# Attention values and exponential sums on one NeuronCore: which operand stands in TensorE and which one moves

## The chip, the cores and the metric

The kernel runs on one NeuronCore of a Trainium2 chip. The metric is the device time of one execution in microseconds, as the median of several runs. Before the change it is 3464.32 us (three runs, 3463.7 to 3466.15).

## The reference, cut to what matters

Two layers of a trunk with three parallel branches (a convolution branch, grouped attention, a long convolution) and a channel mixer. The change concerns the attention of the 1024 latent tokens: 8 heads of 64, 2 groups of keys and values, 1024 own keys and 128 cached ones.

```
def _blocked_attention(q, k, v):
    b, lq, h, d = q.shape
    g = h // N_KV_HEADS
    nb = lq // Q_BLOCK
    qb = q.reshape(b, nb, Q_BLOCK, N_KV_HEADS, g, d).transpose(1, 0, 2, 3, 4, 5)
    scale = d ** -0.5
    def one_block(qi):
        s = jnp.einsum('bqkgd,bskd->bkgqs', qi, k, preferred_element_type=jnp.float32) * scale
        p = jax.nn.softmax(s, axis=-1).astype(v.dtype)
        return jnp.einsum('bkgqs,bskd->bqkgd', p, v)
```

All numbers are fp32. The result of the attention is half of the input of the output projection w_o.

## The kernel before

Activations lie with channels on the 128 partitions and the 1152 tokens (128 context tokens, then 1024 latent ones) in the free dimension. Each layer has four phases: `phase1` (norm, input projection, long convolution), `phase2` (attention, with the convolution branch and the modulation products of later stages beside it), `phase3` (output projection `wo`) and `phase4` (channel mixer `up`, `dn`). The large products of phases 1, 3 and 4 split each fp32 operand into a high and a low part and take three products.

`phase2` (line 1245) opens the pools and calls `attention` (line 1359). Four head pairs `j` (two heads `u` of one key group), two halves of 512 queries and nine chunks `c` of 128 keys make 72 chunks a layer, 144 in all. For one chunk:

- `st`: four products give the scores of 128 keys by 2 x 512 queries, with the row maximum already subtracted through extra rows of the stationary operand; tile `st`, two PSUM banks.
- `p`: one ScalarE exponential over 128 x 1024 (line 1388).
- `av`: `drain` (line 1363) runs two chunks behind. For each head and each block of 128 queries P stands (128 x 128) and the values move: 64 columns and a column of ones, so that column 64 collects the sum of the exponentials. That is eight fp32 products a chunk, accumulated over nine chunks in two PSUM banks.

After chunk 8 `finish` (line 1405) takes the two banks: on VectorE a reciprocal of the sums and a multiplication for each head, then four transposes on TensorE (tile `avt`) bring channels back to the partitions, and `mix_out` (line 1031) splits the result into high and low (ScalarE, VectorE) and stores it to the DRAM buffer `mixD`, from which phase 3 loads it. There are 16 finishes.

Beside this run, as generators that are advanced once a chunk: `maxes` (line 1313) for the next head pair (score products `S`, maxima `mx` on VectorE, transposes `mxt`), `prompt_attention`, `tapped_conv` (the 31-tap convolution on VectorE, ScalarE and GpSimd, then `mu`, `s`, `cr`, `pw` on TensorE) and `mod` (line 352: `cpad` with 32 columns stands, the modulation weights move, four products side by side; tile `modp`). `bcast64` (line 495) makes rows out of columns with pairs of products whose stationary block has 64 columns (tiles `cr`, `nr`).

All products go through one helper (`mm`, line 234), so rows of the profile are told apart by tiles. An fp32 product appears as two matmul instructions in the profile and as one in the program's order. The order of instructions on each engine is set by a scheduler when the program is built (it simulates the time line), not by the order of the lines alone. SP issues nearly all DMAs, in order.

Of the kernel before, what the change touches and what calls it, by code (L numbers as in the profile page):

```python
# [9 lines left out]
F32 = mybir.dt.float32  # L10
# [39 lines left out]
def _constants():  # L50
# [49 lines left out]
        cs[d, 1] = cs[d + 64, 1] = -s if d % 32 < 16 else s  # L100
    c["rope"] = cs.reshape(128, 2 * L)

    m = np.zeros((128, 260), np.float32)
    m[:, :128] = np.eye(128)
    m[:64, 128:192] = 1.0 / 64
    m[64:, 192:256] = 1.0 / 64
    m[:64, 256] = 1.0
    m[64:, 257] = 1.0
    m[:, 258:260] = 1.0 / DM
    c["cst"] = m  # L110
    return c

# [20 lines left out]
class Kern:  # L133
# [171 lines left out]

    def setup(self):
        nc, i = self.nc, self.i
        cst = self.one.tile([128, 260], F32, name="cst")
        nc.sync.dma_start(cst[:], i["cst"])
        self.ident, self.blk, self.sel, self.inv1k = cst[:, :128], cst[:, 128:256], cst[:, 256:258], cst[:, 258:260]  # L310
        self.eps = self.one.tile([128, 2], F32, name="eps")
        nc.vector.memset(self.eps[:, 0:1], EPS)
        nc.vector.memset(self.eps[:, 1:2], 64 * EPS)
        cd = self.one.tile([128, 16], F32, name="cd")
        nc.sync.dma_start(cd[:], i["cond"])
        self.vec = []
# [928 lines left out]
    def phase2(self, l, mods):  # L1245
        nc = self.nc
        with ExitStack() as ctx:
            tp = self.pool(ctx, f"tp{l}", 1)
            self.ap = self.pool(ctx, f"at{l}", 1)
            kp = self.pool(ctx, f"v{l}", 1)  # L1250
            main = {"m": self.pool(ctx, f"g{l}", 5), "t": self.pa}
            side = {"m": self.pool(ctx, f"gc{l}", 3), "t": self.pa}
            self.use(main)
            wm = self.pool(ctx, f"wm{l}", 3)
            self.sq = self.psum(ctx, f"s{l}", 1)

            V = self.V = kp.tile([128, 18, 65], F32, tag="v", name="vt")
            nc.gpsimd.memset(V[:, :, 64:65], 1.0)
            nc.sync.dma_start(V[:, 0:16, 0:64], self.vD[:].rearrange("p a b e -> p (a b) e"))
            nc.sync.dma_start(V[:, 16:18, 0:64], self.i["cv"][l].rearrange("p (b e) -> p b e", b=2))  # L1260
            bgs = [self.stream(self.prompt_attention(l, kp), side), self.stream(self.tapped_conv(l, tp, self.cp), side)]
            if mods is not None:
                bgs.append(self.stream(mods(wm), side))
            self.attention(l, bgs)
            for b in bgs:
                for _ in b:
                    pass
        self.actx.close()
# [90 lines left out]
    def attention(self, l, bgs):  # L1359
# [3 lines left out]
        def drain(n):  # L1363
            while len(pend) > n:
                j, half, c, P = pend.pop(0)
                g = j // 2
                if c == 0:
                    acc[0] = [self.sq.tile([128, 512], F32, tag=f"av{u}", name="av") for u in range(2)]
                for u in range(2):
                    for k in range(4):  # L1370

                        self.mm(acc[0][u][:, 65 * k : 65 * k + 65], P[:, 512 * u + 128 * k : 512 * u + 128 * k + 128], V[:, 2 * c + g, :],
                                c == 0 and k == 0, c == 8 and k == 3)
                if c == 8:
                    fins.append(self.finish(l, j, half, acc[0]))

        Q = self.first
        for j in range(4):
            g = j // 2
            cur, mg, nxt = Q, self.maxes(j + 1) if j < 3 else iter(()), None  # L1380
            for half in range(2):
                for c in range(9):
                    S = self.sq.tile([128, 2, 512], F32, tag="st", name="st")
                    for k, (K, n) in enumerate(((K1[g], 128), (K2[g], 66))):
                        for u in range(2):
                            self.mm(S[:, u, :], K[:n, 128 * c : 128 * c + 128], cur[u][k][:n, 512 * half : 512 * half + 512], k == 0, k == 1)
                    P = ap.tile([128, 1024], F32, tag="p", name="p", bufs=4)
                    self.act(P[:], S[:].rearrange("p a b -> p (a b)"), AF.Exp)
                    nxt = next(mg, nxt)
                    pend.append((j, half, c, P))  # L1390
                    drain(2)
                    for f in fins:
                        next(f, None)
                    for b in bgs:
                        for _ in range(3 if 9 * half + c + 18 * j > 40 else 1):
                            next(b, None)
# [5 lines left out]
            for _ in f:  # L1402
                pass

    def finish(self, l, j, half, av):

        nc = self.nc
        O, rr = self.M("av"), self.small([128, 2, 4, 1], "rs")
        o = O[:].rearrange("p (k u e) -> p u k e", k=4, u=2)
        for u in range(2):  # L1410
            a = av[u][:, 0:260].rearrange("p (k e) -> p k e", e=65)
            nc.vector.reciprocal(rr[:, u], a[:, :, 64:65])
            self.mul(o[:, u], a[:, :, 0:64], rr[:, u].to_broadcast([128, 4, 64]))
        yield
        t = self.T("avt")
        for k in range(4):
            self.tr(t[:, 128 * k : 128 * k + 128], O[:, 128 * k : 128 * k + 128])
        self.mix_out(l, j, t[:], 128 + 512 * half, 640 + 512 * half)
        yield

    def taps(self, l, tp):
# [416 lines left out]
```

## Time and profile before

| | |
|---|---|
| median of the runs | 3464.32 us |
| the profiled execution's own time | 3458.15 us |
| its span | 3456.4 us |
| TensorE, matmul | 94% of the span, 18938 instructions |
| TensorE, weight load | 88% |
| VectorE | 60% |
| ScalarE | 34% |
| mean granted TensorE clock | 0.948 |
| `av` matmuls | 2304 instructions, busy 306.4 us, 285 ns each |
| `av` weight loads | 2304 instructions, busy 312.1 us, 206 ns each |

The profiled execution is one run with the hardware profiler on. Busy time is a union of intervals; a matmul's duration has the time in which its result travels through the array, so matmuls that follow each other overlap in the rows, and the pace is read from the starts. A granted clock of 1.00 is 2.4 GHz and 0.50 is 1.2 GHz.

### The profile page before, as it was taken

The numbers are of one execution on the slowest core, as the hardware profiler recorded it, in microseconds if no ns is written. First come the engines' busy times: TensorE is split into PE (matmuls) and PEld (weight loads), VectorE is DVE, ScalarE is ACT, GpSimd is POOL, SyncE is SP. The second block draws the span as 40 slices with busy tenths as digits, with TensorE's granted clock in tenths as the row PEclk, the third lists the DMA queues.
The fourth block names the chain that finished last, engine by engine and source line by source line (L and its number), as shares of the span: only waits on it lengthen the run. The fifth ranks groups of instructions, "written<-read, shape, count | busy, mean of one in ns | idle before, by whom it ended". The sixth has DMA issues, their size and how long they took to land. (4 is left out here: it accounts for less than half of the span.)

```text
span 3456.4 us, 47618 instructions
## 1 busy us (share of the span) xinstructions
PE 3238.0 (94%) x18938; PEld 3054.2 (88%) x18938; DVE 2074.1 (60%) x3301; ACT 1176.0 (34%) x1944; POOL 568.5 (16%) x498
## 2 busy tenths in 40 slices
PE   5988888999979999999998888989999999999997
PEld 3888866799979999999998888768999999999997
DVE  7877779522775455444566885875146554455556
ACT  3422333342343332233344323425225222333323
POOL 6645421000220000000014662300001000000002
PEclk8999978989989999999999898889999999999998
DMA  7564455434411111111114445433411111111112
GB/s 282 163 208 150 135 153 175 159 113 150 126 56 43 43 41 43 43 43 43 41 49 137 144 117 162 146 128 97 163 46 37 40 43 43 42 41 43 43 41 70
DMA packets 150106, 332.44 MB, mean 96 GB/s; under 512 B 21459, under 2 KB 57687, under 8 KB 143356
## 3 DMA queue, kind: packets, MB, share of 16 engines
q1 hardware_dynamic: 145180, 314.84, 28.6%
q0 software_dynamic: 4704, 14.55, 1.5%
q8 instruction: 150, 2.46, 0.3%
q14 instruction: 72, 0.59, 0.1%
HBM read 261.13 MB, written 68.19 MB: 95 GB/s over the span
## 5 line engine op out<-in xcount | busy, mean ns | idle before, releaser
L234 PE MATMUL up<-hl,whi 128*128 128x384 f32 (+1 forms) x2112 | 713.3, 338 | 4.2 <-DVE hl L223 2.9
L234 PE MATMUL up<-hh,whi 128*128 128x384 f32 (+1 forms) x2112 | 710.8, 338 | 3.7 <-ACT hh L208 2.8
L234 PE MATMUL up<-hh,wlo 128*128 128x384 f32 (+1 forms) x2112 | 712.5, 337 | 0.0
L211 DVE TENSOR_TENSOR wlo<-wraw,whi 128x512 fp32r<-128x512 f32 x296 | 204.5, 691 | 636.6 <-ACT whi L228 636.4
L228 ACT CAST whi<-wraw 128x512 fp32r<-128x512 f32 x362 | 224.1, 619 | 826.3 <-PE dn L234 358.2
L234 PEld LDWEIGHTS up<-hl,whi 128*128 128x128 f32 x2112 | 398.6, 189 | 6.4 <-DVE hl L223 4.7
L234 PEld LDWEIGHTS up<-hh,whi 128*128 128x128 f32 x2112 | 398.6, 189 | 4.4 <-ACT hh L208 3.2
L234 PEld LDWEIGHTS up<-hh,wlo 128*128 128x128 f32 x2112 | 398.6, 189 | 0.0
L223 DVE SCALAR_TENSOR_TENSOR xt<-dn,mod,xt 128x128 f32<-128x128 f32 (+2 forms) x704 | 332.3, 512 | 71.6 <-PE dn L234 71.5
L234 PE MATMUL dn<-gh,wlo 128*128 128x384 f32 (+1 forms) x1056 | 359.0, 340 | 0.0
L234 PE MATMUL dn<-gh,whi 128*128 128x384 f32 (+1 forms) x1056 | 357.2, 338 | 0.0
L234 PE MATMUL dn<-gl,whi 128*128 128x384 f32 (+1 forms) x1056 | 357.0, 338 | 0.0
L234 PEld LDWEIGHTS av<-vt,p 128*128 128x128 f32 x2304 | 312.1, 206 | 21.9 <-issue 5.2
L211 POOL TENSOR_TENSOR acc<-acc,sq 128x384 f32<-128x384 f32 x51 | 55.4, 1095 | 1626.0 <-ACT sq L208 1625.1
L223 DVE SCALAR_TENSOR_TENSOR fu<-pd,vec,fu 128x1154 f32<-128x1154 f32 (+2 forms) x192 | 253.9, 1323 | 91.9 <-ACT fu L208 89.3
L234 PE MATMUL av<-vt,p 128*128 128x65 f32 x2304 | 306.4, 285 | 2.2 <-DVE av L211 2.2
L234 PE MATMUL win<-hh,whi 128*128 128x384 f32 x768 | 270.3, 354 | 27.3 <-ACT raw L724 9.9
L234 PE MATMUL win<-hl,whi 128*128 128x384 f32 x768 | 269.9, 352 | 7.5 <-DVE hl L223 2.9
L234 PE MATMUL win<-hh,wlo 128*128 128x384 f32 x768 | 268.4, 350 | 0.8 <-POOL wlo L211 0.8
L1341 DVE TENSOR_REDUCE mx<-S 128x1 f32<-128x384 f32 x384 | 197.1, 550 | 75.5 <-PE S L234 74.8
L208 ACT ACTIVATE p<-st 128x1024 f32<-128x1024 f32 x144 | 147.3, 1023 | 252.7 <-PE st L234 213.5
L1632 ACT COPY pd<-up 128x384 f32<-128x384 f32 (+1 forms) x352 | 131.5, 400 | 240.2 <-PE up L234 240.2
(282 smaller groups left out, 5414.6 us busy)
## 6 DMA issues: line engine op xcount, KB each, us to landing
wmod<-in_w_mod SPq DMA_DIRECT2D x48, 1024.0 KB, 6.7
wraw<-in_w_up SPq DMA_DIRECT2D x176, 256.0 KB, 2.6
wraw<-in_w_dn SPq DMA_DIRECT2D x88, 256.0 KB, 2.6
wraw<-in_w_in SPq DMA_DIRECT2D x64, 256.0 KB, 2.8
q<-qD SPq DMA_DIRECT2D x48, 256.0 KB, 7.1
mh<-mixD SPq DMA_DIRECT2D x16, 576.0 KB, 4.3
ml<-mixD SPq DMA_DIRECT2D x16, 576.0 KB, 5.9
khD<-fK SPq DMA_DIRECT2D x16, 512.0 KB, 2.9
```

The costliest lines, as they stand in the source:

```text
L208: return self.nc.scalar.activation(out, in_, f, **k)
L211: return (eng or self.nc.vector).tensor_tensor(out, a, b, op=op)
L223: return (eng or self.nc.vector).scalar_tensor_tensor(out, a, s, b, op0=op0, op1=op1)
L228: self.nc.scalar.copy(hi, src)
L234: self.nc.tensor.matmul(out, l, r, start=start, stop=stop)
L1341: nc.vector.tensor_reduce(m3[:, k, s : s + 1], S[:, :384], op=ALU.max, axis=AX.X)
L1632: self.nc.scalar.copy(p[:, u + o : v + o], t[:, u - a : v - a])
```

## The change

The values stand now, 64 columns for one head, and the exponentials move, 512 columns at a time. The two heads of a pair write to the lower and the upper 64 partitions of one PSUM tile (`av`). The sums of the exponentials come from products of their own: a block of 32 columns of ones stands (one element of `eps`, broadcast), P moves, and head and parity of the chunk choose one of four bands of 32 partitions of a second tile (`avs`). The result has channels on the partitions already, so the transposes go. `finish` copies both tiles with ScalarE, and adds the two parities and takes the reciprocal of the sums: for 14 of 16 head pairs and halves by way of DRAM (the four rows are stored, read back as 128 x 8, inverted, stored, and read broadcast over 64 partitions), for the last of each layer with small products (`rs`, then `bcast64`, tile `orr`). P has five buffers instead of four.

```
-            V = self.V = kp.tile([128, 18, 65], F32, tag="v", name="vt")
-            nc.gpsimd.memset(V[:, :, 64:65], 1.0)
+            V = self.V = kp.tile([128, 18, 64], F32, tag="v", name="vt")
...
-                    acc[0] = [self.sq.tile([128, 512], F32, tag=f"av{u}", name="av") for u in range(2)]
+                    acc[0] = [self.sq.tile([128, 512], F32, tag=f"av{u}", name=n) for u, n in enumerate(("av", "avs"))]
+                o, sm = acc[0]
                 for u in range(2):
-                    for k in range(4):
-
-                        self.mm(acc[0][u][:, 65 * k : 65 * k + 65], P[:, 512 * u + 128 * k : 512 * u + 128 * k + 128], V[:, 2 * c + g, :],
-                                c == 0 and k == 0, c == 8 and k == 3)
+                    self.mm(o[64 * u : 64 * u + 64, :], V[:, 2 * c + g, :], P[:, 512 * u : 512 * u + 512], c == 0, c == 8)
+
+                if c % 2 == 0 and c < 8:
+                    acc[1] = P
+                else:
+                    for k, x in enumerate((acc[1], P) if c < 8 else (P,)):
+                        for u in range(2):
+                            r = 64 * k + 32 * u
+                            self.mm(sm[r : r + 32, :], self.ones, x[:, 512 * u : 512 * u + 512], c == 1, c == (7 if k else 8))
                 if c == 8:
-                    fins.append(self.finish(l, j, half, acc[0]))
+                    fins.append(self.finish(l, j, half, acc[0], j == 3 and half == 1))
...
-    def finish(self, l, j, half, av):
+    def finish(self, l, j, half, av, last):
 
         nc = self.nc
-        O, rr = self.M("av"), self.small([128, 2, 4, 1], "rs")
-        o = O[:].rearrange("p (k u e) -> p u k e", k=4, u=2)
-        for u in range(2):
-            a = av[u][:, 0:260].rearrange("p (k e) -> p k e", e=65)
-            nc.vector.reciprocal(rr[:, u], a[:, :, 64:65])
-            self.mul(o[:, u], a[:, :, 0:64], rr[:, u].to_broadcast([128, 4, 64]))
-        yield
-        t = self.T("avt")
-        for k in range(4):
-            self.tr(t[:, 128 * k : 128 * k + 128], O[:, 128 * k : 128 * k + 128])
-        self.mix_out(l, j, t[:], 128 + 512 * half, 640 + 512 * half)
+        O, S = self.M("av"), self.M("sums")
+        nc.scalar.copy(O[:], av[0][:])
+        nc.scalar.copy(S[:], av[1][:])
+        if last:
+            t = self.T("rs")
+            for k in range(4):
+                self.mm(t[:, 2 * k : 2 * k + 2], S[:, 128 * k : 128 * k + 128], self.sel4, True, True)
+            rr = self.small([128, 4, 2], "rs")
+            nc.vector.reciprocal(rr[:], t[:, 0:8].rearrange("p (k u) -> p k u", u=2))
+            R = self.bcast64(rr, 0, 4, "orr")
+        else:
+            d, e = self.dram([2, 2, 512], f"sums{l}{j}{half}"), self.dram([2, 512], f"sumr{l}{j}{half}")
+            nc.sync.dma_start(d[:].rearrange("a u x -> (a u) x"), S[0:128:32, :])
+            n = self.small([128, 2, 8], "ns")
+            for a in range(2):
+                nc.sync.dma_start(n[:, a], d[a].rearrange("u (p e) -> (u p) e", e=8))
+            yield
+            yield
+            self.add(n[:, 0], n[:, 0], n[:, 1])
+            nc.vector.reciprocal(n[:, 0], n[:, 0])
+            nc.sync.dma_start(e[:].rearrange("u (p e) -> (u p) e", e=8), n[:, 0])
+            R = self.M("orr")
+            for u in range(2):
+                nc.sync.dma_start(R[64 * u : 64 * u + 64, :], e[u : u + 1, :].to_broadcast([64, 512]))
+            yield
+            yield
+        self.mul(O[:], O[:], R[:])
+        self.mix_out(l, j, O, 128 + 512 * half, 640 + 512 * half)
         yield
```

The scheduler orders the program anew. On TensorE, late in the first layer's attention, one chunk after the other stands before the change as follows (`st` scores, `av` values; `p_` with its number is the P of the chunk):

```order
L234 MATMUL st_6700<-q1_5977,k1_3589 128x512
L234 MATMUL st_6700<-q1_5982,k1_3589 128x512
L234 MATMUL st_6700<-q2_5978,k2_3592 128x512
L234 MATMUL st_6700<-q2_5983,k2_3592 128x512
L234 MATMUL av_6707<-vt_4248,p_6684 128x65 x4
L234 MATMUL av_6708<-vt_4248,p_6684 128x65 x4
```

In the changed kernel two successive chunks at the same place stand so (`avs` is the tile of the sums, `eps` holds the ones):

```order
L236 MATMUL st_6467<-q1_5857,k1_3590 128x512
L236 MATMUL st_6467<-q1_5862,k1_3590 128x512
L236 MATMUL st_6467<-q2_5858,k2_3593 128x512
L236 MATMUL st_6467<-q2_5863,k2_3593 128x512
L236 MATMUL av_6495<-p_6459,vt_4249 64x512 x2
L236 MATMUL avs_6496<-p_6459,eps_71 32x512 x2
L236 MATMUL st_6488<-q1_5857,k1_3590 128x512
L236 MATMUL st_6488<-q1_5862,k1_3590 128x512
L236 MATMUL st_6488<-q2_5858,k2_3593 128x512
L236 MATMUL st_6488<-q2_5863,k2_3593 128x512
L236 MATMUL av_6495<-p_6472,vt_4249 64x512 x2
L236 MATMUL avs_6496<-p_6472,eps_71 32x512 x2
```

The code issues the sums of an even chunk together with those of the odd one after it; in the built order each chunk's two sums products stand right behind its own two value products. In the whole program they stand 141 times as two in a row and 6 times alone.

On SP's DMA queue, where a head pair's finish and the loads for the last head pair meet in the first layer, the order before is:

```order
L1038 DMA mixD0_107<-mh_5309 128x512
L1039 DMA mixD0_107<-ml_5310 128x512
L1546 DMA mh_6907<-mixD0_107 128x1152
L1547 DMA ml_6908<-mixD0_107 128x1152
L359 DMA wmod_5401<-in_w_mod 128x2048
L359 DMA wmod_5480<-in_w_mod 128x2048
L1321 DMA q1_5977<-qD_109 64x1024 x2
```

and in the changed kernel:

```order
L1324 DMA q1_5862<-qD_110 64x1024 x2
L1325 DMA q2_5863<-qD_110 64x1024
L1429 DMA sums011_5913<-sums_5910 4x512
L1432 DMA ns_5916<-sums011_5913 128x8 x2
L1437 DMA sumr011_5914<-ns_5916 128x8
L1440 DMA orr_5979<-sumr011_5914 64x512
L364 DMA wmod_5243<-in_w_mod 128x2048
L364 DMA wmod_5318<-in_w_mod 128x2048
L1440 DMA orr_5979<-sumr011_5914 64x512
L1043 DMA mixD0_108<-mh_6029 128x512
```

The store and the three kinds of loads of the sums are new, each of them depends on the one ahead of it, and loads of `wmod` stand behind them.

## Rows read from the trace of the kernel before

**Rows 1.** Busy time in six windows: us, PE, PEld, DVE, ACT, POOL, PEclk, DMA share, GB/s

```profile
465.00:600.00 135.00, 118.50 (x678) 92.76 (x677) 119.46 (x220) 49.08 (x72) 32.81 (x25) 0.84 0.46 160
600.00:752.00 152.00, 148.23 (x957) 121.85 (x957) 69.83 (x174) 57.42 (x80) 0.00 (x0) 0.90 0.44 151
752.00:811.00 59.00, 58.56 (x439) 54.95 (x438) 4.79 (x14) 22.65 (x23) 1.05 (x1) 1.00 0.22 72
2155.00:2290.00 135.00, 122.05 (x653) 90.58 (x651) 117.74 (x216) 49.03 (x75) 33.76 (x26) 0.79 0.46 157
2290.00:2424.00 134.00, 130.36 (x905) 113.29 (x906) 72.83 (x173) 56.95 (x79) 0.00 (x0) 0.96 0.30 98
2424.00:2486.00 62.00, 61.27 (x456) 57.42 (x455) 7.11 (x20) 23.25 (x24) 0.00 (x0) 0.99 0.31 111
```

**Rows 2.** The same windows, instructions of tile av alone: us, PE, PEld, DVE

```profile
600.00:752.00 152.00, 68.18 (x477) 68.03 (x477) 3.31 (x12) 0.90 0.44 151
752.00:811.00 59.00, 42.26 (x359) 42.84 (x358) 3.40 (x12) 1.00 0.22 72
...
2290.00:2424.00 134.00, 62.97 (x490) 63.63 (x490) 3.25 (x12) 0.96 0.30 98
2424.00:2486.00 62.00, 43.59 (x364) 44.39 (x364) 3.65 (x12) 0.99 0.31 111
```

**Rows 3.** Timeline of PE late in layer 0: start, us, instruction, count

```profile
770.16 1.18 PE L234 MATMUL st<-q,k 128*128 128x512 f32 x4
771.18 1.90 PE L234 MATMUL av<-vt,p 128*128 128x65 f32 x16
772.88 1.17 PE L234 MATMUL st<-q,k 128*128 128x512 f32 x4
```

**Rows 4.** Busy time in stretches with a granted clock of 0.50, columns of rows 1

```profile
488.50:509.00 20.50, 20.48 (x78) 17.58 (x79) 14.17 (x33) 5.52 (x11) 4.53 (x3) 0.50 0.00 0
...
590.90:607.90 17.00, 17.00 (x71) 13.51 (x70) 10.07 (x21) 1.55 (x2) 0.00 (x0) 0.50 0.44 139
683.00:686.40 3.40, 3.38 (x14) 2.80 (x14) 2.65 (x7) 1.51 (x3) 0.00 (x0) 0.50 0.00 0
730.80:751.30 20.50, 20.50 (x94) 19.66 (x93) 0.69 (x1) 3.10 (x4) 0.00 (x0) 0.50 0.80 300
...
2181.50:2202.00 20.50, 20.50 (x79) 17.62 (x78) 16.19 (x34) 5.26 (x10) 3.75 (x3) 0.50 0.01 1
...
2294.10:2304.40 10.30, 10.20 (x41) 6.79 (x41) 4.61 (x12) 1.07 (x2) 0.00 (x0) 0.50 0.54 166
```

**Rows 5.** Timeline at 730 us, with the idle time before it and its releaser

```profile
730.37 6.29 PE L234 MATMUL av<-vt,p 128*128 128x65 f32 x30 [1.73 <-DVE av L211]
```

**Rows 6.** Timeline of PE around modp, at 477 us and at 2317 us

```profile
476.69 1.06 PE L234 MATMUL modp<-wmod,cpad 128*32 128x512 f32 x8
...
2316.54 1.92 PE L234 MATMUL modp<-wmod,cpad 128*32 128x512 f32 x16
2318.39 0.62 PE L234 MATMUL S<-k,q 128*128 128x384 f32 x2
```

**Rows 7.** Timeline of PE around cr, at 2374 us

```profile
2372.30 2.12 PE L234 MATMUL av<-vt,p 128*128 128x65 f32 x18
2374.35 0.87 PE L234 MATMUL cr<-cst,csd 128*64 128x128 f32 x12
2375.16 3.12 PE L234 MATMUL av<-vt,p 128*128 128x65 f32 x26
```

**Rows 8.** Timeline of PE, two st groups with av and transposes avt between them

```profile
2435.54 1.17 PE L234 MATMUL st<-q,k 128*128 128x512 f32 x4
...
2438.64 1.17 PE L234 MATMUL st<-q,k 128*128 128x512 f32 x4
```

**Rows 9.** Tile modp: a ScalarE copy of 128 x 512 out of PSUM, ns min/median/max

```profile
L368 ACT COPY modm<-modp x6: 567/586/587, 29.6 to 2277.3; 128x512 f32<-128x512 f32 x6
```

**Rows 10.** Tile qp: small loads from DRAM, issue to landing

```profile
DMA to landing us min/median/max: 1.8/2.8/4.2
```

More of the change, by code (lines that the diff above doesn't have):

```diff
@@ L101, in _constants @@
     c["rope"] = cs.reshape(128, 2 * L)
-    m = np.zeros((128, 260), np.float32)
+    m = np.zeros((128, 262), np.float32)
     m[:, :128] = np.eye(128)
@@ L109, in _constants @@
     m[:, 258:260] = 1.0 / DM
+    m[0:128:64, 260] = 1.0
+    m[32:128:64, 261] = 1.0
     c["cst"] = m
@@ L307, in setup @@
         nc, i = self.nc, self.i
-        cst = self.one.tile([128, 260], F32, name="cst")
+        cst = self.one.tile([128, 262], F32, name="cst")
         nc.sync.dma_start(cst[:], i["cst"])
         self.ident, self.blk, self.sel, self.inv1k = cst[:, :128], cst[:, 128:256], cst[:, 256:258], cst[:, 258:260]
-        self.eps = self.one.tile([128, 2], F32, name="eps")
+        self.sel4 = cst[:, 260:262]
+        self.eps = self.one.tile([128, 3], F32, name="eps")
         nc.vector.memset(self.eps[:, 0:1], EPS)
         nc.vector.memset(self.eps[:, 1:2], 64 * EPS)
+        nc.vector.memset(self.eps[:, 2:3], 1.0)
+        self.ones = self.eps[:, 2:3].to_broadcast([128, 32])
         cd = self.one.tile([128, 16], F32, name="cd")
@@ L1255, in phase2 @@
             self.sq = self.psum(ctx, f"s{l}", 1)
-            V = self.V = kp.tile([128, 18, 65], F32, tag="v", name="vt")
-            nc.gpsimd.memset(V[:, :, 64:65], 1.0)
-            nc.sync.dma_start(V[:, 0:16, 0:64], self.vD[:].rearrange("p a b e -> p (a b) e"))
-            nc.sync.dma_start(V[:, 16:18, 0:64], self.i["cv"][l].rearrange("p (b e) -> p b e", b=2))
+            V = self.V = kp.tile([128, 18, 64], F32, tag="v", name="vt")
+            nc.sync.dma_start(V[:, 0:16, :], self.vD[:].rearrange("p a b e -> p (a b) e"))
+            nc.sync.dma_start(V[:, 16:18, :], self.i["cv"][l].rearrange("p (b e) -> p b e", b=2))
             bgs = [self.stream(self.prompt_attention(l, kp), side), self.stream(self.tapped_conv(l, tp, self.cp), side)]
@@ L1386, in attention @@
                             self.mm(S[:, u, :], K[:n, 128 * c : 128 * c + 128], cur[u][k][:n, 512 * half : 512 * half + 512], k == 0, k == 1)
-                    P = ap.tile([128, 1024], F32, tag="p", name="p", bufs=4)
+                    P = ap.tile([128, 1024], F32, tag="p", name="p", bufs=5)
                     self.act(P[:], S[:].rearrange("p a b -> p (a b)"), AF.Exp)
```

## The prediction

> **What bounds the kernel now.** I read the windows of the attention phase first. The change touches that phase alone, once per layer: about 465 to 811 us and 2155 to 2486 us of the span. In the first 135 us of each, VectorE is busy 119.46 and 117.74 us, about 88%: row maxima and the tapped convolution. After that it falls to 70 of 152 us and 5 of 59, and TensorE has the stretch: 148 of 152, 59 of 59, 130 of 134, 61 of 62 us [rows 1]. So the phase has a part paced mostly by VectorE and a part paced by TensorE. The same windows for the tile av say how much of the work lies in the second part: 477, 359, 490 and 364 instructions [rows 2]. A chunk (128 keys for one head pair and 512 queries) has 8 products of two instructions each, so 16: 1690 / 16 = 105.6 of the 144 chunks are paced by TensorE, and 38.4 are not.
>
> The timeline of TensorE shows one chunk where nothing else runs: st starts at 770.16, av at 771.18, the next st at 772.88 [rows 3]. A chunk costs 1.02 + 1.70 = 2.72 us: four 512-column score products, then 16 av instructions with 65 columns moving. The exponential has slack there, at 1.02 us of 2.72.
>
> Last the clock: the granted clock is 0.50 (1.2 GHz) over several stretches inside the phase while TensorE is busy [rows 4]. One of them follows a wait of 1.73 us for VectorE to free the av sums [rows 5].
>
> **The change part by part.** *Values.* Per chunk the 16 instructions with P standing become two products with 64 columns of V standing and P moving, 512 columns each. A product is again two instructions, so 4. Their nearest relative is modp (fp32, 512 columns moving, 32 standing, four products side by side): 8 instructions take 1.06 us and 16 take 1.92 [rows 6]. So a full set of neighbours passes once in 0.86 / 2 = 0.43 us, and a product needs two passes. That 64-column neighbours also run together shows in cr: 12 instructions of 128 columns in 0.87 us [rows 7]; one after another at 0.11 each (a quarter of 0.43) they would need about 1.3 us before the tail of the last. So the av pair costs two passes.
>
> *Sums.* The diff speaks of blocks of 32 ones, four side by side. The scheduled order shows something else: after each av pair stand two sums products of the same P, 141 times "x2" and 6 singles in the whole program, never four. The block for the earlier P is moved ahead of the next av. Two products alone also need two passes, so the sums cost 0.86 us in every chunk, not in every second one.
>
> *Switching.* Going from 128 columns to 128, the next group starts 0.16 to 0.20 us before the last one's end: 771.34 against 771.18, and 773.08 against 772.88 [rows 3]. Between blocks of different width it starts only 0.07 before: 2318.46 against 2318.39 out of modp [rows 6], 2374.42 against 2374.35 into cr and 2375.22 against 2375.16 out of it [rows 7]. A chunk now has three such borders: 128 to 64, 64 to 32, 32 to 128. The trace has no border of 64 to 32; I bound it by 0.07 and 0.16 of overlap and take 0.07, since all borders between widths look so. The Trainium skill (TensorEngine Tiling, Key Properties) says that changing the tiling mode drains the engine, which would hold for 64 to 32 as well; that speaks against this change.
>
> *The chunk after.* st 1.18 - 0.07 = 1.11; av 1.06 - 0.07 = 0.99, and some 0.03 for the wider block to load; sums 1.06 - 0.07 = 0.99. Together 3.12 us against 2.72: **+0.40 us per chunk**. Over 105.6 chunks +42.2 us.
>
> *In VectorE's part* 38.4 x 0.40 = 15.4 us of work is added. It lies between 0 (hidden in VectorE's time) and 15.4; TensorE is busy there 118.50 of 135 us [rows 1], so the two engines share the path, and I take half: +7.7.
>
> *The finish of a head pair.* Four av transposes go. A chunk with them takes 2438.64 - 2435.54 = 3.10 us instead of 2.72 [rows 8], so 0.38 x 11.7 of the 16 finishes that lie in TensorE's part: -4.5. The buffers are freed by two ScalarE copies (0.59 us each [rows 9]; ScalarE is busy 57 of 152 us) instead of four VectorE steps; that takes away the wait of 1.73 us [rows 5]: -1.7. The copies fit beside sums and scores (about 2 us from av's end to the next av). The normalizing multiply, an add and a reciprocal on VectorE stand in for the two reciprocals and two multiplies, about even. The reciprocal of 14 finishes goes through DRAM in four hops at 1.8 to 4.2 us each [rows 10]; nobody on TensorE waits for its result before the output projection, so I cost it at nothing; its cover is the time until the next head pair's loads on SP's queue, and without it the second rival's price applies. The last finish of each layer stays on the chip: 8 small instructions and 16 of cr's kind, at most 0.4 + 0.9 us twice: +2.6.
>
> *The clock.* Five stretches at 0.50 lie on TensorE's path, 20.5 + 17 + 20.5 + 20.5 + 10.3 = 88.8 us, with TensorE busy all but 0.2 us [rows 4]. The shortest stretch of the kind is 3.4 us [rows 4]. If each shrank to that, (88.8 - 17) / 2 = 36 us come back (the same work takes half). The new av and sums stream 512 columns where 65 stood, and the wait ahead of the fourth goes, so I expect shorter stretches; no row shows how the new mix behaves. Bounds 0 and -36; I take -20.
>
> *Sum:* 42.2 + 7.7 - 4.5 - 1.7 + 2.6 - 20 = **+26 us**. The profiled execution took 3458.15 us, so 3484; the median of the runs shown is 6.2 us above it, so I say **3490 us**. By the ends: 42.2 + 15.4 - 4.5 + 2.6 = +56 (3520) and 42.2 - 4.5 - 1.7 - 36 - 105.6 x 0.09 (no drain from 64 to 32) = -9.5 (3455).
>
> **The rivals.** *The clock pays for it (faster or level).* Place: the stretches at 1.2 GHz. With about 36 us back and the first part hidden by VectorE, the sum is 42 - 6 + 3 - 36 = +3, and -7 with a free 64 to 32 border; it turns to a gain once more than 46 us of waits and slow clock vanish. For it: the stretch from 731 us opens with 30 av instructions and stays at 1.2 GHz for 20.5 us with TensorE always busy [rows 4, 5]. Against: what VectorE does in the first part stays as it was, and so do TensorE's waits for it. Time: 3455 to 3470.
>
> *SP's queue holds things up (slower still).* SP issues in order; the new reads of DRAM wait for writes just issued, and behind them stand wmod loads and the next pair's q. If each of 14 finishes costs TensorE one wait of 1.3 us or more, +18: 3508; with waits that lower the clock again, past 3520.
>
> *The change does what it says.* With four sums side by side, two chunks would cost 4.26 (st and av twice) + 0.99 = 5.25 us, 2.63 each, and the total would be about 105.6 x -0.09 - 4.5 - 20, some -35 us: 3430. The order on record excludes it, unless the hardware joins pairs over an av that lies between. The Trainium skill (TensorEngine Tiling, Theoretical Speedup) gives up to 4x for operands of 32; by this order only two of the four blocks are ever in use.
>
> **How the numbers follow.** A measurement of this kernel can tell about 0.2%, 7 us, from no change. Forecast (+8 to +56): 0.68, all slower. Clock rival 0.22: 0.11 faster, 0.11 within. SP rival or a worse clock, past +56: 0.08. Four side by side: 0.02. So faster 0.13, within 0.11, slower 0.76. The range 3455 to 3520 takes in the forecast's case and about two thirds of the clock rival's: 0.82.
>
> **What would show it.** Right: away from other work a chunk of about 3.1 us with av and sums at 1.0 each, both as groups of four instructions; overlap of 0.07 at all three borders; no av transposes; the two attention phases together 15 to 50 us longer and the rest unchanged; ScalarE at about a third of a chunk. Wrong: sums or av taking 1.8 us per chunk (the neighbours do not run together; +0.86 a chunk each), chunks at 2.7 or less, or a granted clock of 1.0 over the whole phase.

## The result, and the profile after

The change makes the kernel faster by 0.56%: 3444.03 us against 3464.01 us (medians of four runs each, measured together), ratio 0.9944 with a 95% interval of 0.9929 to 0.9960. The forecast was 3490 us, slower by 0.7%. The profiled execution took 3443.87 us (span 3441.6, mean granted clock 0.962; before 3458.15, 3456.4 and 0.948). All ratios here and below leave out runs that took over 1.5% more than the shortest of their kernel (two of four of e3_p5, one of four of e2_actfree, one of ten of e5_ones64).

Only the two attention phases differ by much. The windows of the kernel before, from the first exponential of each layer's attention to its first `wo` product (window, length, then busy us and instructions of PE, PEld, DVE, ACT, POOL, then PEclk, DMA share, GB/s):

```profile
462.20:811.70 349.50, 328.50 (x2084) 272.00 (x2083) 197.12 (x415) 130.41 (x177) 35.11 (x27) 0.89 0.41 141
...
2152.70:2486.00 333.30, 315.81 (x2020) 263.06 (x2020) 199.20 (x412) 130.45 (x181) 33.99 (x27) 0.90 0.36 124
2486.00:3452.20 966.20, 945.68 (x5402) 942.85 (x5400) 514.85 (x772) 315.02 (x524) 38.92 (x39) 0.99 0.16 49
```

The same windows of the changed kernel:

```profile
463.60:790.30 326.70, 320.18 (x1482) 133.15 (x1480) 197.20 (x400) 137.28 (x192) 34.12 (x27) 0.97 0.46 158
...
2131.10:2467.00 335.90, 320.89 (x1420) 133.44 (x1420) 199.55 (x401) 139.02 (x197) 33.42 (x27) 0.95 0.38 129
2467.00:3437.70 970.70, 950.02 (x5418) 946.78 (x5417) 516.09 (x774) 315.11 (x524) 36.88 (x39) 0.99 0.16 48
```

The two phases go from 682.8 to 662.6 us, by 20.2; the last stage takes 4.5 us longer, which I cannot place. TensorE is busy in all of them, and what changed is the clock column: 0.89 and 0.90 became 0.97 and 0.95. The idle time (length less PE) went from 21.0 + 17.5 to 6.5 + 15.0 us.

The chunk itself is what was forecast. TensorE's timeline of the changed kernel where nothing else runs (start, us of the group, instruction, count; compare [rows 3]):

```profile
755.52 1.10 PE L236 MATMUL st<-q,k 128*128 128x512 f32 x4
756.55 1.08 PE L236 MATMUL av<-p,vt 128*64 128x512 f32 x4
757.57 1.05 PE L236 MATMUL avs<-p,eps 128*32 128x512 f32 x4
758.55 1.21 PE L236 MATMUL st<-q,k 128*128 128x512 f32 x4
759.68 1.08 PE L236 MATMUL av<-p,vt 128*64 128x512 f32 x4
760.69 1.05 PE L236 MATMUL avs<-p,eps 128*32 128x512 f32 x4
761.67 0.50 PE L236 MATMUL st<-q,k 128*128 128x512 f32 x1
```

From 758.55 to 761.67 is 3.12 us, with 1.13 for `st`, 1.01 for `av` and 0.98 for the sums. The chunk ahead of it takes 3.03: its `st` does not follow a group of sums and needs only 1.03. The sums stand in twos, never in fours.

The stretches at half the clock, to be held against [rows 4] (same columns as the windows), with the long stretch at full clock behind the last one of each layer:

```profile
545.20:555.40 10.20, 9.86 (x23) 3.91 (x22) 10.20 (x17) 7.03 (x12) 9.56 (x7) 0.50 0.50 185
562.20:569.00 6.80, 6.72 (x16) 2.27 (x16) 3.96 (x7) 1.02 (x1) 0.84 (x1) 0.50 0.01 2
569.00:790.30 221.30, 220.61 (x1075) 93.79 (x1074) 104.99 (x233) 89.34 (x120) 1.05 (x1) 1.00 0.47 162
2132.40:2135.80 3.40, 3.40 (x9) 1.14 (x7) 2.47 (x9) 1.88 (x4) 0.00 (x0) 0.51 0.00 0
2173.30:2180.10 6.80, 5.67 (x13) 2.22 (x14) 5.94 (x15) 2.40 (x4) 0.00 (x0) 0.50 0.00 0
2217.70:2227.90 10.20, 8.11 (x31) 2.72 (x31) 10.09 (x20) 4.61 (x7) 4.74 (x3) 0.50 0.51 161
2231.30:2241.50 10.20, 8.02 (x18) 3.26 (x18) 9.46 (x14) 6.99 (x11) 6.37 (x4) 0.50 0.23 88
2241.50:2467.00 225.50, 223.68 (x1044) 95.81 (x1042) 108.42 (x241) 92.04 (x124) 2.02 (x2) 1.00 0.36 121
```

Together 47.6 us at 1.2 GHz, in six stretches; the kernel before has eleven that begin in the two phases, 146.8 us, five of which stand in [rows 4] as the ones that I counted. They begin behind waits in both kernels. The waits of TensorE in the first phase, before (engine, waiting tile, what it waited for: us, times, longest):

```profile
PE S L234 <- DVE mx L1341: 3.9, 4, 2.0
PE mxt L244 <- DVE nmx L223: 3.8, 1, 3.8
...
PE av L234 <- DVE av L211: 1.7, 1, 1.7
```

and after:

```profile
PE S L236 <- DVE mx L1344: 3.3, 3, 2.5
PE sp L236 <- DVE modm L213: 1.0, 1, 1.0
```

The wait of 2.5 us for `mx` ends at 562.3, and 6.8 us at half the clock follow. Before the change a wait of 1.97 us for `mx` (486.6 to 488.5) was followed by 20.5 us, and the 1.73 us of [rows 5] by another 20.5.

### The profile page after: what moved, and what is told of

Same layout as the page of the kernel before. It is cut to its first block, busy times and chain, and to the rows that moved or that the text cites. A ratio compares the mean times of both kernels' runs of the same rounds, so it can differ in the third digit from the quotient of the medians.

```text
span 3441.6 us, 45444 instructions
## 1 busy us (share of the span) xinstructions
PE 3239.8 (94%) x17770; PEld 2791.8 (81%) x17770; DVE 2080.7 (60%) x3284; ACT 1192.0 (35%) x1976; POOL 565.2 (16%) x496
## 5 line engine op out<-in xcount | busy, mean ns | idle before, releaser
L236 PEld LDWEIGHTS dn<-gh,wlo 128*128 128x128 f32 x1056 | 199.9, 189 | 0.0
L236 PEld LDWEIGHTS dn<-gh,whi 128*128 128x128 f32 x1056 | 199.2, 189 | 0.0
```

The costliest lines, as they stand in the source:

```text
L236: self.nc.tensor.matmul(out, l, r, start=start, stop=stop)
```

## The account of the two phases, for all kernels

Three numbers of each profile split a phase's length: TensorE's idle time, the time at half the clock (what lies inside the phases of the stretches at 1.2 GHz; before, 146.4 of the 146.8 us above, since one runs in from the stage ahead and one runs out; the expectations below count only stretches that begin in a phase, 181 us instead of 194.5 for e3_p5), and the work, which is busy time less half the time at half the clock, that is, the busy time had the clock stayed at 2.4 GHz (the idle bits inside those stretches, a few us, count as work here). Sums over both phases, us:

| kernel | profiled execution | phases | idle | at half clock | work |
|---|---|---|---|---|---|
| before | 3458.2 | 682.8 | 38.5 | 146.4 | 571.1 |
| after | 3443.9 | 662.6 | 21.5 | 47.6 | 617.3 |
| e1_wide (before, 128 columns) | 3428.7 | 652.9 | 46.7 | 57.9 | 577.2 |
| e8_w96 (before, 96 columns) | 3430.4 | 652.4 | 38.0 | 81.1 | 573.8 |
| e3_p5 (before, 5 buffers) | 3487.1 | 711.0 | 46.4 | 194.5 | 567.3 |
| e9_wide_p5 (both of these) | 3429.7 | 648.9 | 44.2 | 60.2 | 574.6 |
| e2_actfree (before, copies) | 3434.9 | 661.1 | 31.8 | 135.8 | 561.4 |
| e7_both (128 columns, copies) | 3403.4 | 628.1 | 28.3 | 51.0 | 574.3 |
| e6_dvecopy (after) | 3437.1 | 651.2 | 19.7 | 29.3 | 616.9 |
| e11_after_p4 (after) | 3440.9 | 663.6 | 22.5 | 41.7 | 620.2 |
| e5_ones64 (after) | 3470.2 | 671.6 | 40.8 | 66.6 | 597.5 |
| e4_four (after) | 3382.0 | 602.4 | 30.3 | 30.6 | 556.8 |
| e10_four_dve (after) | 3378.6 | 601.7 | 29.9 | 37.4 | 553.1 |

From before to after: work +46.2, idle -17.0, clock (47.6 - 146.4) / 2 = -49.4, together -20.2. The change does add work, as forecast, and more than that comes back through the clock.

The scheduler builds another order for every one of these kernels, so none differs from the kernel before in its edit alone. But the time at half the clock falls into groups by the columns that move in a value product, whatever the order: 135.8 to 194.5 us in the three kernels with 65 columns, 51.0 to 81.1 in the four with 96 or 128, 29.3 to 66.6 in the six with 512.

## The experiments

Theory A: the clock. While value products move 65 columns behind a weight load of 128 columns, TensorE is busy and its clock stays low; the changed kernel moves 512 columns instead, so a fall of the clock after a wait is short. Theory B: the waits. The sums' buffers come free earlier, so there are fewer falls.

### Columns alone: e1_wide

```
-            V = self.V = kp.tile([128, 18, 65], F32, tag="v", name="vt")
-            nc.gpsimd.memset(V[:, :, 64:65], 1.0)
+            V = self.V = kp.tile([128, 18, 128], F32, tag="v", name="vt")
+            nc.gpsimd.memset(V[:, :, 64:128], 1.0)
...
-                        self.mm(acc[0][u][:, 65 * k : 65 * k + 65], P[...
+                        self.mm(acc[0][u][:, 128 * k : 128 * k + 128], P[...
```

(Both long lines are cut at the end; the finish reads blocks of 128 columns instead of 65.)

Expected: 

> The kernel before, with one edit: 128 columns move instead of 65 in every value product (the columns of ones are repeated). The weight load of 128 columns sets the pace there (0.112 us an instruction), and 128 moving columns fit into the same time (a quarter of 0.43 us is 0.107), so at full clock a chunk should stay at 2.72 to 2.8 us. Theory A (clock): the gain of the change comes from columns that stream through the array, which bring the clock back soon after a wait; then stretches at 1.2 GHz inside the two attention phases shrink from about 150 us to under 60, and the time falls to 3420 to 3445 us. Theory B (waits): the gain comes from value buffers that ScalarE frees instead of VectorE, so TensorE waits less; then this edit does nothing, 3458 to 3470 us, with the slow stretches as long as before.

Measured 3426.96 us against 3464.55 (ratio 0.9893, 0.9861 to 0.9925). With 63 idle columns more in each value product, and the order that the scheduler makes of it, the kernel before is faster than the changed one. Its two phases:

```profile
465.40:793.80 328.40, 305.31 (x2084) 249.03 (x2083) 197.40 (x414) 130.26 (x177) 34.94 (x27) 0.96 0.44 151
...
2132.40:2456.90 324.50, 300.91 (x2020) 250.24 (x2020) 197.69 (x412) 131.09 (x181) 33.38 (x27) 0.95 0.37 127
```

Same instruction counts as before, work and idle time a little higher (6 and 8 us), and 88 us less at half the clock. The other runs say the same: span times granted clock, an estimate of the span at full clock, is 3283 to 3297 us in its four runs and 3275 to 3283 in the twelve of the kernel before beside them, so what was gained is clock. At the place of [rows 5], the timeline reads:

```profile
722.31 3.62 PE L234 MATMUL av<-vt,p 128*128 128x128 f32 x30 [0.53 <-DVE av L211]
```

Thirty instructions take 3.62 us here, at full clock, and 6.29 before, though they move twice the columns. The waits ahead are shorter here (0.60 and 0.53, 1.73 before), so this one place does not decide it; a pair with equal waits stands below, under e7_both.

### Half of it: e8_w96

The same edit with 96 columns instead of 128.

Expected: 

> The kernel before with value blocks of 96 columns moving, half way between its 65 and the 128 of the wide run; the added columns are more ones. Theory A, if the clock follows the columns gradually: a gain of 12 to 25 us, 3440 to 3452. If it is all or nothing: near the wide run (3422 to 3432) or near the kernel before (3458 to 3466). Theory B expects nothing of it: 3458 to 3466, since the waits stay.

Measured 3431.7 us (ratio 0.9909, 0.9875 to 0.9943): at the upper edge of the wide run's band. The time at half the clock is 146.4, 81.1 and 57.9 us with 65, 96 and 128 columns: half the added columns bring three quarters of it. Theory B has nothing to offer for this run; its waits are those of before (38.0 us).

### A buffer more, without and with columns: e3_p5, e9_wide_p5

```
-                    P = ap.tile([128, 1024], F32, tag="p", name="p", bufs=4)
+                    P = ap.tile([128, 1024], F32, tag="p", name="p", bufs=5)
```

In e3_p5 this is the only edit to the kernel before; in e9_wide_p5 it stands beside that of e1_wide.

Expected: 

> The kernel before with five buffers for the exponentials instead of four, the smallest piece of the change alone. Theory A: no column more is streamed, so the half-clock stretches stay, 3455 to 3470, within 7 us of the kernel before. Theory B in its wider form (any buffer that comes free earlier helps): exponentials run further ahead of the value products, TensorE waits less than 21 and 18 us in the two phases, 3430 to 3450.

Expected: 

> The kernel before with value blocks of 128 columns (the wide run: 3427, 45 to 55 us of the phases at half the clock) and five buffers for the exponentials instead of four, which alone made the kernel before slower (3486 and more in its profiled run: 181 us at half the clock instead of 147). Theory A (what five buffers cost is clock: waits are followed by longer stretches at 1.2 GHz where value products of 65 columns stand in a row): with 128 columns that loss is gone, 3415 to 3435. Rival (the other order that five buffers bring costs by itself, in waits or work): the loss of 25 us or more stays, 3450 or above.

e3_p5 is slower, which neither theory expected: ratio 1.0136 (1.0047 to 1.0225), and 3487, 3530, 3541 and 3551 us in its four runs, the profiled one being the shortest. Span times granted clock is 3279 to 3289 us in all four (3272 to 3286 for the kernel before beside them): the loss, and its spread, is clock. The scheduler uses the fifth buffer to put more value products in a row. TensorE's timeline there:

```profile
749.59 5.06 PE L234 MATMUL av<-vt,p 128*128 128x65 f32 x30 [1.73 <-DVE av L211]
...
755.29 7.35 PE L234 MATMUL av<-vt,p 128*128 128x65 f32 x34
762.40 2.05 PE L234 MATMUL st<-q,k 128*128 128x512 f32 x4
764.25 5.21 PE L234 MATMUL av<-vt,p 128*128 128x65 f32 x24
```

and the stretch at half the clock behind that wait, in columns of the windows:

```profile
751.40:795.80 44.40, 44.40 (x188) 41.81 (x188) 2.60 (x6) 8.51 (x10) 0.00 (x0) 0.50 0.36 135
```

The wait is the 1.73 us of [rows 5], the stretch 44.4 us instead of 20.5, with TensorE busy throughout.

e9_wide_p5 tells whether the fifth buffer costs anything but clock: 3427.2 us (ratio 0.9889, 0.9862 to 0.9916), what e1_wide takes. With 128 columns moving, five buffers cost nothing. Its long rows of value products run at full clock right behind two waits, which are shorter than that of e3_p5:

```profile
683.75 0.44 PE L234 MATMUL S<-k,q 128*128 128x384 f32 x1 [0.56 <-DVE mx L1341]
684.98 0.41 PE L234 MATMUL pw<-cxh,whi 128*128 128x384 f32 x1 [0.79 <-DVE ml L211]
...
686.11 2.62 PE L234 MATMUL av<-vt,p 128*128 128x128 f32 x22
```

### The buffers freed by copies: e2_actfree, e7_both, e6_dvecopy

e2_actfree gives the kernel before the changed kernel's way of freeing the sums; e7_both has that and 128 columns:

```
             a = av[u][:, 0:260].rearrange("p (k e) -> p k e", e=65)
...
+            C = self.ap.tile([128, 260], F32, tag="avc", name="avc", bufs=2)
+            nc.scalar.copy(C[:], av[u][:, 0:260])
+            a = C[:].rearrange("p (k e) -> p k e", e=65)
```

Expected: 

> The kernel before, with one edit: after chunk 8 ScalarE copies each bank of value sums (128 x 260) to SBUF, and VectorE's reciprocals and multiplications read the copy, so that the bank is free without VectorE. Theory B (waits): TensorE's idle time in the attention phases (21 and 17 us) falls to that of the changed kernel (7 and 15), fewer stretches at 1.2 GHz follow, and the time falls to 3440 to 3452 us. Theory A (clock): the waits may shorten, but the slow stretches that open for other reasons stay long; 3453 to 3468 us.

Expected: 

> The kernel before with both single edits that gained: value blocks widened from 65 to 128 columns moving, and the value sums copied to SBUF by ScalarE. If theory A and theory B are two separate gains (37 and 34 us by their own runs) they add up: 3390 to 3400. If both buy back the same stretches at half the clock, of which the kernel before has some 140 us in the two phases (worth 70 us) and the wide blocks alone leave 45: between 3410 and 3428, with the granted clock of the phases at 0.97 or above.

e2_actfree: ratio 0.9897 (0.9857 to 0.9938), three runs of 3422 to 3435 us, below both bands, and one of 3477. The gain is in the second layer (333.3 to 314.0 us; the first 349.5 to 347.1), and the order of TensorE's work changed widely with the edit, so it proves little by itself. e7_both: 3401.67 us (ratio 0.9829, 0.9787 to 0.9871), 1.7 us outside the band for adding up (3390 to 3400), which its interval overlaps, and below the band for one and the same gain. Against e1_wide its phases are 24.8 us shorter: 18.4 from idle time (46.7 to 28.3), 3.5 from the clock (57.9 to 51.0 us at half), 2.9 from work. So early copies do take away idle time in the old form, some 18 us, for the most part beside the clock and not through it.

The two runs also hold the plainest evidence for theory A. Late in the first layer TensorE waits 2.16 us in both, for the same VectorE step and at the same place of the program (behind 236 instructions of `st` and 864 of `av`), and transposes and a long row of value products follow. Beside the columns, only the order behind it and the width of ScalarE's copies (512 columns for 260) differ. In e2_actfree (65 columns; the timeline behind the wait, then the stretch in the columns of the windows):

```profile
744.63 0.98 PE L244 MATMUL avt<-cst,av 128*128 128x128 f32 x4 [2.16 <-DVE av L211]
745.41 7.35 PE L234 MATMUL av<-vt,p 128*128 128x65 f32 x34
744.80:792.60 47.80, 47.80 (x200) 45.19 (x199) 3.90 (x10) 9.77 (x13) 0.00 (x0) 0.50 0.45 161
```

In e7_both (128 columns):

```profile
735.27 0.63 PE L244 MATMUL avt<-cst,av 128*128 128x128 f32 x4 [2.16 <-DVE av L211]
735.73 5.14 PE L234 MATMUL av<-vt,p 128*128 128x128 f32 x30
736.60:740.00 3.40, 3.40 (x18) 3.40 (x17) 1.31 (x3) 0.00 (x0) 0.00 (x0) 0.51 0.98 280
740.00:782.40 42.40, 42.40 (x326) 40.13 (x325) 2.59 (x6) 17.05 (x19) 1.05 (x1) 1.00 0.57 206
```

After the same wait TensorE is busy without a gap in both, for 47.8 us at 1.2 GHz with 65 columns, and for 3.4 us at 1.2 GHz and 42.4 at 2.4 GHz with 128.

e6_dvecopy asks whether that depends on ScalarE:

```
-        nc.scalar.copy(O[:], av[0][:])
-        nc.scalar.copy(S[:], av[1][:])
+        nc.vector.tensor_copy(O[:], av[0][:])
+        nc.vector.tensor_copy(S[:], av[1][:])
```

Expected: 

> The changed kernel with the two copies that free the av and avs sums done by VectorE instead of ScalarE, all else the same. VectorE is the engine that is late in the first part of each phase. Theory A (the gain is clock, brought by the 512 columns that now stream): TensorE's work and the columns are the same, so the granted clock of the two phases stays at about 0.97 and 0.95, and the time within 8 us of the changed kernel's: 3436 to 3452. Theory B (the gain comes from buffers freed by ScalarE): the waits for VectorE's copies return, TensorE is idle 20 us or more in the first phase instead of 6.5, each wait lowers the clock again, and the time goes back to 3455 to 3470, near the kernel before.

Measured 3431.89 us (ratio 0.9906, 0.9871 to 0.9941; the changed kernel has 0.9944, 0.9929 to 0.9960), below both bands. The copies on the engine that was said to be late cost nothing: idle time 19.7 us against 21.5, time at half the clock 29.3 against 47.6. Theory B in the form "ScalarE is free, VectorE is late" falls. That the second phase's falls of the clock become shorter here (30.6 to 13.6 us) comes with a new order; why just these is open.

### The fifth buffer of the changed kernel: e11_after_p4

`bufs=5` back to `bufs=4` in the changed kernel.

Expected: 

> The changed kernel with four buffers for the exponentials, as before, instead of five; each pair of sums needs the exponentials of two chunks, so a buffer is held longer. Theory A (columns streamed decide the clock, buffers don't): 3436 to 3455, granted clock of the two phases 0.95 or above. Rival (the fifth buffer is needed, since one P waits for its partner's sums): TensorE waits for the exponentials in many of the 144 chunks, 0.2 us or more each, 3470 or above.

Measured 3443.03 us (ratio 0.9944, 0.9923 to 0.9965), the changed kernel's ratio. In this form the fifth buffer does nothing.

### The price of the borders, and VectorE: e5_ones64

```
-        self.ones = self.eps[:, 2:3].to_broadcast([128, 32])
+        self.ones = self.eps[:, 2:3].to_broadcast([128, 64])
...
+                for u in range(2):
+                    self.mm(sm[64 * u : 64 * u + 64, :], self.ones, P[:, 512 * u : 512 * u + 512], c == 0, c == 8)
...
+        nc.vector.reciprocal(R[:], av[1][:])
```

Sums come out on all 64 partitions of a head; the trip through DRAM and the copy of the sums go.

Expected: 

> The changed kernel, with blocks of 64 ones: the sums of every chunk go to the same two bands of 64 partitions, stand there broadcast already, and the reciprocal is taken from PSUM by VectorE; no trip through DRAM, no rs or orr. The border from 64 to 32 columns goes. If that border costs the 0.1 us a chunk that the prediction took (0.07 us of overlap instead of about 0.16), a chunk falls from 3.13 to about 3.02 and the time by 8 to 16 us, to 3428 to 3436. If the border were free and the trips through DRAM hidden, 3440 to 3448 us. If the reciprocal over 512 columns on VectorE holds up the buffers, above 3448 us.

Measured 3469.24 us (ratio 1.0017, 0.9999 to 1.0036), 3470.23 in the profiled execution: the last of the three cases, and not the gain of the border alone. The chunk does get shorter, by its timeline:

```profile
786.68 1.20 PE L236 MATMUL st<-q,k 128*128 128x512 f32 x4
787.82 1.08 PE L236 MATMUL av<-p,vt 128*64 128x512 f32 x4
788.73 1.03 PE L236 MATMUL avs<-p,eps 128*64 128x512 f32 x4
789.68 1.20 PE L236 MATMUL st<-q,k 128*128 128x512 f32 x4
```

3.00 us from `st` to `st`, and the sums start 0.17 before the end of `av` (788.73 against 788.90) where the changed kernel has 0.06 (757.57 against 757.63). So the border from 64 to 32 columns costs 0.1 us a chunk. What eats it in the two phases is, as far as the waits show, the reciprocal on VectorE (duration min/median/max in ns):

```profile
L1414 DVE RECIPROCAL orr<-avs x16: 3343/3357/3358, 512.1 to 2488.2; 128x512 f32<-128x512 f32 x16
```

16 x 3.36 = 54 us on the engine that paces the first part. TensorE's idle time goes from 21.5 to 40.8, in the first layer 9.0 of it for the maxima `mx` (3.3 in the changed kernel), and the time at half the clock from 47.6 to 66.6; together with 19.8 us less work this makes the phases 9.0 us longer. The rest of the 26 us between the two profiled executions lies in other stages (1348.4 us between the phases against 1340.8, for one), which I cannot explain.

This run is also a control for theory B in the new form. TensorE idles 40.8 us in its phases, as much as before the change (38.5), and is still at half the clock for 66.6 us only, instead of 146.4. So 40 of the 49 us that the clock gave the changed kernel come in this form without its shorter idle time. A changed kernel with fewer columns moving was not tried.

### Four sums that really stand side by side: e4_four, e10_four_dve

The two chunks of a pair share one P tile, and each sums product reads a quarter of the columns (256 queries of one head) of both chunks, so that all four blocks depend on the same exponentials and stand together:

```
-                    P = ap.tile([128, 1024], F32, tag="p", name="p", bufs=5)
+                    if c % 2 == 0:
+                        P = ap.tile([128, 2, 1024], F32, tag="p", name="p", bufs=3)
...
+                if c % 2 == 1:
+                    for u in range(2):
+                        for q in range(2):
+                            r = 64 * u + 32 * q
+                            i = 512 * u + 256 * q
+                            self.mm(sm[r : r + 32, :], self.ones, PP[:, :, i : i + 256], c == 1, False)
```

(after chunk 8 the same four with 256 columns each; the finish adds the two halves as it did the two parities). e10_four_dve has VectorE do the two copies of its finish, as in e6_dvecopy.

Expected: 

> The changed kernel, with sums that really stand four side by side: each of the four products reads 256 queries of the even and 256 of the odd chunk, so that all four become ready with the odd chunk, and the built order has them four in a row. By the rows a pair of chunks costs 2 x 2.13 + 0.99 = 5.25 us instead of 6.26, 0.5 us less a chunk. Theory A and the sum of the prediction agree here: with TensorE pacing 100 to 110 chunks at full clock, 3444 falls by 40 to 55, to 3390 to 3405 us. Rival C: once TensorE is lighter, VectorE (row maxima, convolution) or the loop of scores and exponential paces the phases, and only half comes back, 3412 to 3430 us.

Expected: 

> The version with four sums side by side (3385) with the two copies of the finish on VectorE instead of ScalarE, which took 12 us off the changed kernel. If that gain was idle time of TensorE in the second phase and clock after it (16 of 336 us idle there, 31 us at half the clock), little of it is left to gain here (17 us at half the clock): 3375 to 3388. If ScalarE's copies are what holds the exponentials up, the whole gain returns: 3368 to 3376. If VectorE becomes the bound, as the shorter phase leaves it less room: 3390 or above.

e4_four: 3384.6 us (ratio 0.9780, 0.9742 to 0.9818), better than both kernels and a little better than the band. Its timeline:

```profile
742.66 1.06 PE L237 MATMUL avs<-p,eps 128*32 128x512 f32 x8
743.66 1.21 PE L237 MATMUL st<-q,k 128*128 128x512 f32 x4
744.79 1.08 PE L237 MATMUL av<-p,vt 128*64 128x512 f32 x4
745.98 1.21 PE L237 MATMUL st<-q,k 128*128 128x512 f32 x4
747.12 1.08 PE L237 MATMUL av<-p,vt 128*64 128x512 f32 x4
748.12 1.06 PE L237 MATMUL avs<-p,eps 128*32 128x512 f32 x8
```

Four products (eight instructions) take 1.00 us from start to the next `st`, where two took 0.98 (760.69 to 761.67 in the changed kernel); from one group of sums to the next, two chunks, it is 5.46 us, 2.73 a chunk, as much as in the kernel before (2.72). The Trainium skill (TensorEngine Tiling, Theoretical Speedup) gives up to 4x for operands of 32; the trace agrees in that four take 1.00 us where two took 0.98, once the program puts four there. The work falls by 60.5 us against the changed kernel. e10_four_dve: 3385.63 us (ratio 0.9765, 0.9736 to 0.9794), the same: little time at half the clock was left to gain, as expected.

## Why the prediction was wrong

**Right: the chunk.** 3.12 us were forecast and 3.12 measured; `av` 1.02 forecast, 1.01 measured; sums 0.99 and 0.98; `st` 1.11 and 1.13. All three borders overlap by 0.06 to 0.08 us in the timeline, as taken from `modp` and `cr` [rows 6, 7]; e5_ones64 shows 0.17 with equal widths. That is the drain of which the Trainium skill speaks (TensorEngine Tiling, Key Properties); the trace agrees, at 0.1 us a border. The reading of the order, two sums and not four, was right as well, and the other order is worth 60 us (e4_four).

**Near in sum, partly by luck: the added work.** 42.2 + 7.7 - 4.5 + 2.6 = 48.0 us forecast, 46.2 measured. But the table counts the work of all 144 chunks and 16 finishes, hidden or not; counted so, the forecast was 144 x 0.40 - 16 x 0.38 + 2.6 = 54.1, and 7.9 too much. Where these were saved is open.

**Wrong, the main step: "The clock. ... Bounds 0 and -36; I take -20."** Measured -49.4. The mechanism was in the text, its size was not, for two reasons that the trace of before could have told. First, only five stretches with 88.8 us were counted as lying on TensorE's path; the phases hold eleven with 146.8 us, and in those that I left to VectorE's part TensorE was busy too (11.33 of 13.7 us at 553.3, 23.57 of 27.3 at 2239.5). By the prediction's own formula, each shrinking to 3.4 us, all eleven give (146.8 - 37.4) / 2 = 54.7 us, not 36. The clock column of the whole phases, 0.89 and 0.90, warns of it in one line: 0.11 x 349.5 + 0.10 x 333.3 is some 72 us, all that the clock could give back. Second, half of the bound was taken for want of a row. The old form's products are 65 columns behind loads of 128; [rows 4] had TensorE busy 20.5 of 20.5 us without the clock coming back, and that was reason enough to expect that a form with 512 columns leaves such stretches. That the columns do it, and not the waits, is shown in the old form by e1_wide and e8_w96 (only the columns edited), by the equal waits of e2_actfree and e7_both, and by e3_p5 against e9_wide_p5: a buffer that lengthens the rows of value products costs 1.4% with 65 columns moving and nothing with 128. In the new form e5_ones64 shows that most of the gain is there without shorter waits.

**Wrong, a second step: idle time.** I took the wait of [rows 5] away (-1.7) and put half of the chunks' extra 15.4 us into VectorE's part as new time (+7.7, in the sum above). Idle time fell by 17.0 instead: by 10.7 in VectorE's part of the first layer (up to 600 us), not at all in that of the second (up to 2290 before, 2268 after), and by 6.4 in TensorE's parts. That the early copies help is shown for the old form (e7_both against e1_wide, 18 us of idle time); how the 17 us divide between them and the longer chunk, which may fill gaps in which TensorE used to wait, was not tried apart.

These make up the error, in the terms of the table: 29.4 from the clock (-20 forecast, -49.4 measured), 9.2 from idle time (26.3 - 54.1 + 20 = -7.8 forecast, -17.0 measured) and 7.9 from the work, 46.5 in all, which is what lies between +26.3 forecast and -20.2 measured for the phases.

**The rivals.** "The clock pays for it" is what happened; it asked for more than 46 us of waits and slow clock to vanish, and 66.4 did. Its time, 3455 to 3470, was too long for the same reason as above. "SP's queue holds things up" did not come: the loads of the sums and what waited for them read

```profile
  DMA ns<-sums: 36.4, 7
who waited for it (us, times):
  DVE ns L213: 36.4, 7
  PEld S L236: 1.9, 3
```

VectorE stands 36.4 us in seven waits for them (and 19.2 us in seven more for the rows that come back as `orr`), and the weight loads of TensorE that wait for `ns` lose 1.9 us over the whole program. "The change does what it says" needed another program (e4_four), at 3384.6 us instead of the 3430 that I gave it; here too the clock makes the difference.

## What to carry to other kernels

Read the granted clock of a whole phase before pricing an edit there: (1 - clock) x length is what the clock alone can give back, 72 us here, and the 49 that came paid for the 46 us of added work. A product that loads 128 columns to move 65 may be free to widen: here 65, 96 and 128 moving columns took the same time at full clock, and with more columns the stretches at half the clock were shorter. And look in the built order for blocks meant to run side by side; if they depend on different inputs, the scheduler may part them, and a layout in which all of them need the same input puts them together.

## What was not expected of the hardware

- The price of a wait depends on what runs after it: waits of 1.73 us were followed by 20.5 us (before) and 44.4 us (e3_p5) at 1.2 GHz with 65-column products; a wait of 2.16 us by 47.8 us with 65 columns (e2_actfree) and by 3.4 us with 128 (e7_both), a wait of 2.53 us by 6.8 us in the changed kernel.
- Value products with 128 columns moving instead of 65 cost no more: 1.70 us for 16 at full clock before [rows 3] and 1.70 in e1_wide (from 772.58 to 774.28 us), and the work of the phases differs by 6 us of 571 for twice the columns.
- VectorE's reciprocal took 3.36 us on 128 x 512 and 0.20 us on 128 x 8 (the changed kernel's `ns`): the trip through DRAM that makes the small shape possible lets VectorE wait, and TensorE hardly (1.9 us of its weight loads).
- One buffer more made the kernel before 1.4% slower (e3_p5), and with 128 columns moving it cost nothing (e9_wide_p5).
